# Two gathered steps moved from the v stage to the u stage of a product-key mixer, with later waits on ScalarE and eight weight tiles asked for later

## The chip, the cores and the metric

The kernel runs on one core of one Trainium2 chip. The metric is the device time of one execution in microseconds (us), from the first to the last instruction of the program with what lies around them. Engines are named as in the profile: PE (TensorE matmuls), PEld (its weight loads), DVE (VectorE), ACT (ScalarE), POOL (GpSimd), SP (SyncE, which only issues transfers here). The times below come from three timed executions and from one execution under the profiler.

## The reference

A decoder trunk of two layers over 256 positions of 1024 floats. Layer 0 has an attention and retention mixer, layer 1 a short gated convolution, and each is followed by the channel mixer in which this change lies, an expert retrieval with product keys (PEER):

```python
q = (t @ w_q).reshape(n_tok, PEER_HEADS, 2, PEER_DKEY // 2)          # 8 heads
sc = jnp.einsum('thpd,hpnd->thpn', q, sub_keys)                       # 2 x 128 keys a head
s1, i1 = lax.top_k(sc[:, :, 0], 16)
s2, i2 = lax.top_k(sc[:, :, 1], 16)
cand = s1[..., :, None] + s2[..., None, :]                            # sums of pairs
top_s, pos = lax.top_k(cand, 16)                                      # 16 experts a head
gate = jax.nn.softmax(top_s, axis=-1)
hid = jax.nn.gelu(jnp.einsum('td,thkd->thk', tc, u[ec]))              # rows of u, 16384 x 1024
out = jnp.einsum('thk,thkd->td', gc * hid, v[ec])                     # rows of v, 16384 x 1024
```

So each of 256 tokens needs 128 rows of `u` and the same 128 rows of `v`, with a softmax gate a row. Weights and activations are 32-bit floats.

## The kernel before, in words

**Two ways to the experts.** The first 96 tokens are done by gathering: 96 steps fetch, by an indirect transfer that POOL issues, 128 rows of `u` (one for each partition, 128x1024 floats, 0.524 MB), and DVE multiplies them with the tokens and adds up (line 1043); 96 further steps fetch 128 rows of `v`, which DVE adds into three accumulators with the gate times the hidden value as factor (line 1054). The text calls each of these 192 steps a row. The other 160 tokens go through every expert: the u stage multiplies 128 tiles of `u` (128x1024 floats each) with the tokens on PE (line 1449), ACT applies the gelu (line 1489) and the gates come in later; the v stage multiplies 128 tiles of `v` with the gated hidden values (lines 1555, 1589, 1591). The two ways run side by side: `ga.rate` says how many rows are taken a tile of the u stage, and what is left over is spread evenly over the v stage. `UPTO` is the number of rows, one figure a layer, that are to be done when tile 117 of the u stage is reached (after it the rate is 0.6).

**The order.** Each engine's queue is written out by hand, in the order of the program; nothing is moved by a scheduler. A step of the u stage is: eight double matmuls of tile `i`, the gelu of its 128x160 result on ACT, then whatever the work list (`Pump`) has credit for, then the rows that `ga.rate` has credit for. PE writes the results of successive tiles to four accumulators in turn (`acc` twice, `hid` twice).

**Before the gates.** The work list holds the choice of experts for the 256 tokens in two halves (`th`): the top 16 of each of the 16 score vectors (`stage1`), the candidates of four heads at a time (`stage2_build`, nine broadcast sums after a cast of the indices), their top 16 (`stage2_top`), and the way back from positions to indices (`extract`), all on DVE. Its entries have a cost, and each step gives 1.4 of credit, so an entry `(3.0, None)` is a pause. The softmax is cut in three: `gates` (DVE subtracts the maximum), `gates_exp` (ACT, which loads the table of the exponential for it and then that of the gelu again, lines 1277 and 1489) and `gates_norm` (DVE). The gathered rows have such a pair as well: `later` puts the gelu of 32 hidden values on ACT (line 1049) two rows after the last of them, and the product with the gates on DVE two rows after that. When the list is empty, the gates proper begin: one-hot matrices on DVE, their scaling on ACT (lines 1397 and 1400), small matmuls `G` on PE and a product with the hidden values on DVE (line 1492 for each later tile), in 40 groups over the rest of the u stage.

**Transfers.** SP's queue loads the tiles of `u` and `v` in pairs (1 MB) into a ring of eight tiles, `raw`, each when its place is free. 31 of the 128 tiles of `u` (`PRE`) have places elsewhere, in memory that is not yet or no longer used. Eight of these become free only when the query projection ends, and are asked for at tile 0 (six of them, `early_u`) and at tiles 1 and 2 (`early_ko`).

## Time and profile before

| | |
|---|---|
| median of 3 runs | 1441.81 us (1440.76 to 1442.34) |
| the profiled execution | 1445.61 us, of which the span is 1443.5 us |
| granted PE clock | 0.998 |
| busy share of the span | PE 98%, PEld 93%, DVE 86%, ACT 54%, POOL 49% |
| moved by DMA | 532.28 MB, 369 GB/s over the span |
| u stage, layer 0 and 1 | about 180 to 488 us and 882 to 1185 us from the span's start |
| v stage, layer 0 and 1 | about 488 to 727 us and 1185 to 1425 us |

The rest of the span is the two mixers, the query projections (131 to 180 us and 828 to 882 us) and the last norm. The table of the page says little about the change, since PE looks busy nearly everywhere; the windows by stage and the waits by stage say more. "Waited for" names the instruction that came last before a wait ended. Idle times under 150 ns are not listed among the waits.

### The profile page before, as it was taken

What the parts mean: (1) busy time and instruction counts of PE and PEld (TensorE: products, weight loads), DVE (VectorE), ACT (ScalarE), POOL (GpSimd) and SP (SyncE); (2) the same over time, 40 slices, a digit from 0 to 9 for tenths busy, and PEclk for the clock granted to TensorE, in tenths of its full rate; (3) what the DMA queues carried; (4) which work ended last, traced back from release to release, by engine and by line L of the source; (5) the groups of instructions that cost most, each with busy time, mean ns of one, the idle gap of its engine ahead of it and who ended that gap; (6) DMA issues with size and microseconds to landing.
All of it is one profiled execution on the core that took longest, in us unless ns stands there. A gap on an engine that the chain in (4) does not pass through costs nothing.

```text
span 1443.5 us, 30069 instructions
## 1 busy us (share of the span) xinstructions
PE 1414.7 (98%) x11368; PEld 1343.9 (93%) x11376; DVE 1238.9 (86%) x2520; ACT 775.9 (54%) x1820; POOL 703.0 (49%) x495
## 2 busy tenths in 40 slices
PE   9999999999999999999999999999999999999898
PEld 6679999999999999999999999999999999999897
DVE  6638998978889799999987699998888978999896
ACT  6555412148787455655654452212887845655554
POOL 5753633565555343443236363356665644445440
PEclk9999999999999999999999999999999999999999
DMA  9657899999999999999977599999999999999994
GB/s 371 228 158 255 316 409 396 400 395 413 410 413 404 401 406 415 414 415 414 412 267 238 194 324 377 413 409 383 411 414 412 409 392 412 415 416 414 415 415 173
DMA packets 115361, 532.28 MB, mean 369 GB/s; under 512 B 13008, under 2 KB 13264, under 8 KB 86544
## 3 DMA queue, kind: packets, MB, share of 16 engines
q1 hardware_dynamic: 58320, 325.05, 57.4%
q0 software_dynamic: 56032, 203.74, 35.6%
q8 instruction: 89, 1.46, 0.4%
q10 hardware_dynamic: 864, 1.57, 0.3%
q14 instruction: 56, 0.46, 0.1%
HBM read 528.97 MB, written 1.05 MB: 367 GB/s over the span
## 4 chain that ended last, share of the span: by engine, by line
PE 59%; DMA 17%; DVE 17%; issue 3%; ACT 2%; POOL 1%; DVEq 0%; ACTq 0%; SPq 0%; POOLq 0%
PE hid L1449 25%; PE vo L1589 9%; DMA raw<-pv 8%; DMA rows<-pvn,ig 5%; PE vo L1591 4%; PE hid L324 4%; PE vo L1555 4%; DVE gacc L1054 2%; PE hid L330 2%; DVE vlo L1467 2%; PE G L1407 2%; DVE rows L1043 1%; DMA raw<-ew_in 1%; PE ea L356 1%; PE ea L357 1%
## 5 line engine op out<-in xcount | busy, mean ns | idle before, releaser
L1449 PE MATMUL hid<-xf,raw 128*128 128x160 f32 x3104 | 444.9, 300 | 2.8 <-DVE hg L1492 2.3
L1449 PEld LDWEIGHTS hid<-xf,raw 128*128 128x128 f32 x3104 | 426.3, 190 | 4.0 <-DVE hg L1492 3.3
L1460 ACT CAST vhi<-raw 128x1024 fp32r<-128x1024 f32 x212 | 217.9, 1048 | 197.1 <-DMA raw<-pv 127.8
L1033 POOL DMA_INDIRECT rows<-pvn,ig x128 | 192.2, 1502 | 205.7 <-DVE gacc L1054 159.9
L1467 DVE TENSOR_TENSOR vlo<-raw,vhi 128x1024 bf16<-128x1024 f32 x212 | 255.7, 1220 | 33.9 <-ACT vhi L1460 32.8
L1033 POOL DMA_INDIRECT rows<-pun,ig x128 | 159.6, 1247 | 147.6 <-DVE rows L1043 74.7
L194 POOL TENSOR_TENSOR lo<-raw,hi 128x1024 bf16<-128x1024 f32 x67 | 161.2, 2422 | 83.6 <-ACT hi L190 61.4
L1589 PE MATMUL vo<-ko,vhi 128*128 128x320 f32 x1120 | 199.0, 320 | 0.4 <-ACT vhi L1460 0.4
L1043 DVE SCALAR_TENSOR_TENSOR rows<-rows,xg 128x1024 f32<-128x1024 f32 x128 | 154.8, 1218 | 20.9 <-DMA rows<-pun,ig 20.7
L1589 PEld LDWEIGHTS vo<-ko,vhi 128*128 128x128 f32 x1120 | 165.6, 188 | 1.0 <-ACT vhi L1460 1.0
L1489 ACT ACTIVATE hg<-hid 128x160 f32<-128x160 f32 (+14 forms) x240 | 62.4, 265 | 193.4 <-PE hid L1449 193.2
L1054 DVE SCALAR_TENSOR_TENSOR gacc<-rows,ghid,gacc 128x1024 f32<-128x1024 f32 x124 | 158.5, 1278 | 9.1 <-DMA rows<-pvn,ig 8.9
L1591 PE MATMUL vo<-hb,vlo 128*128 128x160 bf16 x1696 | 154.1, 234 | 8.3 <-DVE vlo L1467 7.9
L1033 POOL DMA_INDIRECT grow<-pvn,ig x64 | 90.1, 1407 | 113.1 <-DVE gacc L1054 88.6
L1591 PEld LDWEIGHTS <-vlo 128*128 128x128 bf16 x1696 | 112.1, 98 | 32.9 <-DVE vlo L1467 13.2
L1397 ACT ACTIVATE ko<-ko,idxT 128x128 f16<-128x128 f16 x320 | 101.7, 391 | 32.4 <-DVE ko L1382 32.2
L190 ACT CAST hi<-raw 128x1024 fp32r<-128x1024 f32 (+1 forms) x101 | 103.3, 1043 | 28.7 <-PE hid L324 16.6
L1555 PE MATMUL vo<-hg,raw 128*128 128x160 f32 x704 | 106.9, 302 | 3.1 <-DVE hg L1492 3.1
L324 PE MATMUL hid<-x,hi 128*128 128x256 f32 x800 | 107.4, 287 | 0.8 <-DVE cg L970 0.8
L1033 POOL DMA_INDIRECT grow<-pun,ig x64 | 73.6, 1150 | 70.8 <-DVE grow L1043 29.3
L1589 PE MATMUL vo<-xf,vhi 128*128 128x320 f32 x576 | 102.5, 320 | 0.4 <-ACT vhi L1460 0.4
L1400 ACT ACTIVATE ko<-ko,idxT 128x128 f16<-128x128 f16 x320 | 101.2, 388 | 0.0
(266 smaller groups left out, 2302.5 us busy)
## 6 DMA issues: line engine op xcount, KB each, us to landing
raw<-pv SPq DMA_DIRECT2D x128, 1024.0 KB, 10.4
raw<-pu SPq DMA_DIRECT2D x96, 1024.0 KB, 8.2
raw<-wq SPq DMA_DIRECT2D x32, 512.0 KB, 4.3
hg<-pe_ SPq DMA_DIRECT2D x28, 512.0 KB, 6.6
raw<-ew_in SPq DMA_DIRECT2D x25, 512.0 KB, 6.0
raw<-ow_in SPq DMA_DIRECT2D x24, 512.0 KB, 5.5
raw<-ew_out SPq DMA_DIRECT2D x8, 512.0 KB, 4.5
raw<-ow_out SPq DMA_DIRECT2D x8, 512.0 KB, 4.5
```

Source lines behind the costliest of these rows:

```text
L190: self.nc.scalar.copy(hi[:, c], t[:, c])
L194: eng.tensor_tensor(lo[:, c], t[:, c], hi[:, c].bitcast(F32), OP.subtract)
L324: pe.matmul(ps[:, :S], hi[:, k * P:(k + 1) * P], A2[:, k, s_, :], start=k == 0 and s_ == 0, stop=False)
L1033: gp.indirect_dma_start(self.row(s_), None, table, bass.IndirectOffsetOnAxis(IG[:, 0, s_ % STEPS:s_ % STEPS + 1].bitcast(U32), 0))
L1043: v.scalar_tensor_tensor(r, r, 1.0, XG[:, 0, :], op0=OP.mult, op1=OP.mult, accum_out=w)
L1054: v.scalar_tensor_tensor(self.acc[q], r, w, self.acc[q], op0=OP.mult, op1=OP.add)
L1449: pe.matmul(ps[:, :TD], w[k], xv["xf"][:, k, :], start=k == 0, stop=k == ND - 1)
L1460: act.copy(whi[j], raw)
L1467: v.tensor_tensor(wlo[j], raw, whi[j].bitcast(F32), OP.subtract)
L1555: pe.matmul(vo[b][:, TG:S], w[:, c], HG[:, i, :], stop=i == NK - 1, **m)
L1589: pe.matmul(vo[b][:, TG:S + TD], hi[:, b * P:(b + 1) * P], hs, **m)
L1591: pe.matmul(vo[b][:, TG:S], lo[:, b * P:(b + 1) * P], hb, **m)
```

## The change

It has five parts.

1. `ga.rate` before the gates is 0.95 rows a tile instead of 0.9 (tiles 8 to 57), and `UPTO` is 123 and 121 instead of 121 and 119: two more rows a layer are done in the u stage, two fewer in the v stage.
2. The candidates of the second token half (`th` = 1) are made by ACT, head by head (`head_build`, nine small activations with a bias, and a cast after the fourth head), in place of two `stage2_build` on DVE. `cand` and `IF` get three buffers instead of one.
3. `gates_exp(0)` comes eight tiles later, `gates_exp(1)` follows `gates(1)` by two pauses instead of one, and the gelu of 32 gathered hidden values comes twelve rows after the last of them instead of two (the product with the gates after sixteen instead of four).
4. The eight tiles of `u` that were asked for at tiles 0, 1 and 2 are asked for one at a time at tiles 2, 10, 16, 21, 26, 31, 36 and 41 (`LATER`), each 24 to 66 tiles before its use.
5. The list of work before the gates is 2.0 shorter in cost (the two builds), so the gates begin sooner.

The same matmuls are made, and the same bytes are moved.

ACT's queue of layer 0 before, from the tiles just ahead of the gelu of the first 32 gathered hidden values (`ghid`) to the exponential of the second token half (`hg` there is the scratch in which the gates lie; `hid` are the accumulators):

```order
L1489 ACTIVATE hg_1301<-hid_2766 128x160
L1489 ACTIVATE hg_1301<-hid_2779 128x160
L1049 ACTIVATE ghid_1306<-ghid_1306 128x32
L1489 ACTIVATE hg_1301<-hid_2794 128x160
L1489 ACTIVATE hg_1301<-hid_2811 128x160
L1489 ACTIVATE hg_1301<-hid_2825 128x160
L1489 ACTIVATE hg_1301<-hid_2839 128x160
L1489 ACTIVATE hg_1301<-hid_2852 128x160
L1277 ACT_TABLE_LOAD
L1277 ACTIVATE hg_1301<-hg_1301,nw_174 128x128
L1489 ACT_TABLE_LOAD
```

The same place now, where the line of the exponential is 1294, of the gelu of a tile 1509 and of `ghid` 1050:

```order
L1509 ACTIVATE hg_1301<-hid_2906 128x160
L1509 ACTIVATE hg_1301<-hid_2918 128x160
L1294 ACT_TABLE_LOAD
L1294 ACTIVATE hg_1301<-hg_1301,nw_174 128x128
L1509 ACT_TABLE_LOAD
L1509 ACTIVATE hg_1301<-hid_2931 128x160
L1509 ACTIVATE hg_1301<-hid_2944 128x160
L1509 ACTIVATE hg_1301<-hid_2956 128x160
L1050 ACTIVATE ghid_1306<-ghid_1306 128x32
L1509 ACTIVATE hg_1301<-hid_2969 128x160
```

The gelu of `ghid` has moved behind the exponential. One of the eight places at which ACT now makes candidates, behind tile 28 of layer 0 (one head is nine activations, lines 1211 and 1212; a cast of the indices follows the fourth and the eighth head):

```order
L1509 ACTIVATE hg_1301<-hid_2618 128x160
L1211 ACTIVATE hg_1301<-hg_1301 128x16
L1211 ACTIVATE hg_1301<-hg_1301 128x8
L1211 ACTIVATE hg_1301<-hg_1301 128x5
L1211 ACTIVATE hg_1301<-hg_1301 128x4
L1211 ACTIVATE hg_1301<-hg_1301 128x3
L1211 ACTIVATE hg_1301<-hg_1301 128x2 x3
L1212 ACTIVATE hg_1301<-hg_1301 128x8
L1509 ACTIVATE hg_1301<-hid_2641 128x160
```

Before, only the gelus stood there, and DVE had nine sums and a cast for four heads at once. SP's queue from the end of the query projection of layer 0, before (the names are where a tile of `u` goes):

```order
L161 DMA raw<-pu 128x2048
L1143 DMA hg_1301<-pe_ 128x1024 x2
L1143 DMA xg<-pe_ 128x1024
L1143 DMA ulo_2101<-pe_ 128x512
L1143 DMA one_1312<-pe_ 128x512
L1143 DMA uhi_2104<-pe_ 128x1024
L1143 DMA uhi_2106<-pe_ 128x1024
L1143 DMA xb<-pe_ 128x1024
L1143 DMA uhi_2109<-pe_ 128x1024
L1143 DMA ulo_2111<-pe_ 128x512
L1143 DMA ulo_2112<-pe_ 128x512
L1143 DMA ko_2130<-pe_ 128x1024 x2
```

and now, up to the fifth of the eight:

```order
L162 DMA raw<-pu 128x2048
L1144 DMA hg_1301<-pe_ 128x1024 x2
L1144 DMA xg<-pe_ 128x1024
L1144 DMA ko_2132<-pe_ 128x1024
L162 DMA raw<-pu 128x2048 x3
L1144 DMA ko_2132<-pe_ 128x1024
L162 DMA raw<-pu 128x2048 x2
L1144 DMA ulo_2372<-pe_ 128x512
L1144 DMA one_1312<-pe_ 128x512
L162 DMA raw<-pu 128x2048 x2
L1144 DMA uhi_2475<-pe_ 128x1024
L162 DMA raw<-pu 128x2048 x2
```

The eight stand between pairs of the ring now, not ahead of all of them. The diff, cut to its core:

```diff
-UPTO = (121, 119)
+UPTO = (123, 121)
...
+LATER = dict(zip((2, 10, 16, 21, 26, 31, 36, 41), [i for i in sorted(PRE) if 14 <= PRE[i] < 22]))
...
-                    self.later[s_ + 2] = lambda: act.activation(w, w, AF.Gelu)
-                    self.later[s_ + 4] = lambda: v.tensor_tensor(w, w, g, OP.mult)
+                    self.later[s_ + 12] = lambda: act.activation(w, w, AF.Gelu)
+                    self.later[s_ + 16] = lambda: v.tensor_tensor(w, w, g, OP.mult)
...
-            IF = scr(half).bitcast(F16)
-            cand = scr(PH // 2 * NC)
+            IF = [scr(half).bitcast(F16) for _ in range(3)]
+            cand = [scr(PH // 2 * NC) for _ in range(3)]
...
-            early_u = [i for i in sorted(PRE) if 14 <= PRE[i] < 20]
-            early_ko = [i for i in sorted(PRE) if 20 <= PRE[i] < 22]
...
+            def part(th, hf):
+
+                return th * (1 + hf)
...
+            def head_build(th, hh):
+                def g():
+                    o = hh * 2 * TK
+                    s1, s2 = V[th][:, o:o + TK], V[th][:, o + TK:o + 2 * TK]
+                    cc = cand[part(th, hh // HH)][:, hh % HH * NC:(hh % HH + 1) * NC]
+                    mid = TK // 2
+                    for a in range(mid):
+                        w = WIDTHS[a]
+                        act.activation(cc[:, STARTS[a]:STARTS[a] + w], s2[:, :w], AF.Identity, bias=s1[:, a:a + 1])
+                    act.activation(cc[:, STARTS[mid]:], s1[:, mid:], AF.Identity, bias=s2[:, 0:1])
+                    if hh % HH == HH - 1:
+                        n = NPAIR * TK // 2
+                        act.copy(IF[part(th, hh // HH)], IU[th][:, hh // HH * n:(hh // HH + 1) * n].bitcast(U32))
+                return g
...
             def chain(th, hf):
-                pump.add((1.0, stage2_build(th, hf)))
+                if th == 0:
+                    pump.add((1.0, stage2_build(th, hf)))
...
-                pump.add(*[(2.7, stage1(1, f, f + 2)) for f in range(HH * 2, NPAIR, 2)])
-                pump.add((0.0, lambda: gates_exp(0)))
+                for h in range(HH):
+                    f = (HH + h) * 2
+                    pump.add((2.7, stage1(1, f, f + 2)), (0.0, head_build(1, h)))
                 chain(1, 0)
+                for h in range(HH):
+                    pump.q.insert(len(pump.q) - 6 + h, (0.0, head_build(1, HH + h)))
+                pump.q.insert(len(pump.q) - 2, (0.0, lambda: gates_exp(0)))
                 pump.add((0.6, lambda: gates_norm(0)), (0.3, shares))
                 chain(1, 1)
-                pump.add((0.3, lambda: gates(1)), (3.0, None), (0.0, lambda: gates_exp(1)), (3.0, None),
-                         (0.6, lambda: gates_norm(1)), (3.0, None), (3.0, None), (0.5, idx_tr), (3.0, None))
+                pump.add((0.3, lambda: gates(1)), (3.0, None), (3.0, None), (0.0, lambda: gates_exp(1)),
+                         (3.0, None), (0.6, lambda: gates_norm(1)), (3.0, None), (0.5, idx_tr), (3.0, None))
...
-                    for k in early_u:
-                        fetch(k)
-                elif early_ko:
-                    fetch(early_ko.pop(0))
+                if i in LATER:
+                    fetch(LATER[i])
...
-                ga.rate = (0.9 if 8 <= i < 58 else 0.6) if gst["g"] < 0 else (UPTO[l] - ga.c) / (NK - CALM - i) if i < NK - CALM else 0.6
+                ga.rate = (0.95 if 8 <= i < 58 else 0.6) if gst["g"] < 0 else (UPTO[l] - ga.c) / (NK - CALM - i) if i < NK - CALM else 0.6
```

More of the change, by code (lines that the diff above doesn't have):

```diff
@@ L1183, in peer @@
             HH = PH // 2
+            def part(th, hf):
+                return th * (1 + hf)
             def stage2_build(th, hf):
                 def g():
-                    hs = slice(hf * HH, (hf + 1) * HH)
                     n = NPAIR * TK // 2
-                    v.tensor_copy(IF, IU[th][:, hf * n:(hf + 1) * n].bitcast(U32))
-                    vv = V[th].rearrange("p (h s k) -> p h s k", h=PH, s=2)[:, hs]
-                    cc = cand.rearrange("p (h n) -> p h n", h=HH)
+                    v.tensor_copy(IF[part(th, hf)], IU[th][:, hf * n:(hf + 1) * n].bitcast(U32))
+                    vv = V[th].rearrange("p (h s k) -> p h s k", h=PH, s=2)[:, hf * HH:(hf + 1) * HH]
+                    cc = cand[part(th, hf)].rearrange("p (h n) -> p h n", h=HH)
                     for a in range(TK // 2):
@@ L1206, in g @@
                         to = (th * PH + hh) * TK
-                        todo.append((top[:, to:to + TK], PU[:, o * TK:(o + 1) * TK], cand[:, o * NC:(o + 1) * NC]))
+                        todo.append((top[:, to:to + TK], PU[:, o * TK:(o + 1) * TK], cand[part(th, h0 // HH)][:, o * NC:(o + 1) * NC]))
                     top16(todo)
@@ L1228, in extract @@
                 hs = slice(hf * HH, (hf + 1) * HH)
-                ii = IF.rearrange("p (h s k) -> p h s k", h=HH, s=2)
+                ii = IF[part(th, hf)].rearrange("p (h s k) -> p h s k", h=HH, s=2)
                 def of(t):
```

## The prediction

> **What bounds the kernel now.** The page says first that PE leaves little:
>
> ```profile
> span 1443.5 us, 30069 instructions
> PE 1414.7 (98%) x11368; PEld 1343.9 (93%) x11376; DVE 1238.9 (86%) x2520; ACT 775.9 (54%) x1820; POOL 703.0 (49%) x495
> ```
>
> So I went to the windows by stage (stretch, length, busy us of PE, PEld, DVE, ACT, POOL, granted clock, DMA share, GB/s), layer 0 and then layer 1:
>
> ```profile
> 180.00:240.00 60.00, 60.00 (x445) 60.00 (x444) 54.93 (x218) 13.27 (x34) 21.31 (x21) 1.00 1.02 409
> 240.00:260.00 20.00, 20.00 (x149) 20.00 (x148) 19.76 (x81) 2.74 (x9) 11.48 (x9) 1.00 0.98 382
> 260.00:280.00 20.00, 19.49 (x144) 19.25 (x143) 19.69 (x75) 2.52 (x10) 12.22 (x13) 1.00 1.02 406
> 280.00:300.00 20.00, 18.17 (x134) 17.93 (x133) 17.16 (x33) 5.08 (x11) 10.44 (x10) 1.00 0.98 383
> 300.00:320.00 20.00, 20.00 (x154) 19.96 (x154) 16.71 (x32) 8.84 (x33) 14.92 (x12) 1.00 1.02 401
> 320.00:476.00 156.00, 154.23 (x1300) 152.03 (x1299) 135.01 (x256) 121.52 (x465) 88.23 (x73) 1.00 1.02 409
> 488.00:727.00 239.00, 234.90 (x2021) 221.66 (x2022) 219.17 (x208) 141.88 (x177) 87.38 (x59) 1.00 1.01 411
> 882.00:980.00 98.00, 98.00 (x724) 98.00 (x723) 95.07 (x372) 17.92 (x51) 41.87 (x41) 1.00 1.02 410
> 980.00:1000.00 20.00, 20.00 (x149) 20.00 (x148) 16.29 (x34) 5.79 (x13) 13.23 (x10) 1.00 0.96 361
> 1000.00:1160.00 160.00, 160.00 (x1349) 158.51 (x1348) 137.01 (x264) 124.98 (x477) 99.97 (x75) 1.00 1.02 412
> 1185.00:1420.00 235.00, 228.89 (x1974) 216.61 (x1975) 218.00 (x207) 139.81 (x175) 102.28 (x61) 1.00 1.01 413
> ```
>
> Three things are to be seen. DMA moves 409 to 413 GB/s all through both stages, except in a hole before the gates (382, 406, 383 and 401 in layer 0, 361 in layer 1): there, as I read it, the ring is full and the rows wait for DVE. DVE is nearly full before the gates (95.07 of 98 us) and in the v stage (219 of 239, 218 of 235). PE idles in layer 0 at 260 to 300 us, and in both v stages. What it waited for there, the waits of PE by stage say (180 to 300, 300 to 488, 488 to 727, 1000 to 1185 and 1185 to 1420 us; in 882 to 1000 there is none):
>
> ```profile
> PE hid L1449 <- ACT hg L1489: 2.3, 2, 1.8
> PE hid L1449 <- DVE hg L1492: 1.8, 3, 1.1
> PE vo L1591 <- DVE vlo L1467: 2.4, 6, 0.7
> PE vo L1555 <- DVE hg L1492: 1.6, 1, 1.6
> PE hid L1449 <- DVE hg L1492: 0.5, 1, 0.5
> PE vo L1591 <- DVE vlo L1467: 5.5, 7, 1.9
> ```
>
> The 2.3 us are two late gelus, and the timeline of ACT has their causes, first in layer 0, then the same two places in layer 1:
>
> ```profile
> 278.68 0.23 ACT L1049 ACTIVATE ghid<-ghid 128x32 f32<-128x32 f32 x1 [8.39 <-DVE rows L1043]
> 281.95 1.28 ACT L1277 ACT_TABLE_LOAD   x1
> 290.04 0.40 ACT L1277 ACTIVATE hg<-hg,nw 128x128 f32<-128x128 f32 x1 [6.81 <-DVE hg L1273]
> 290.46 1.28 ACT L1489 ACT_TABLE_LOAD   x1
> ...
> 964.90 0.30 ACT L1489 ACTIVATE hg<-hid 128x160 f32<-128x160 f32 x1 [1.87 <-PE hid L1449]
> 967.07 0.30 ACT L1489 ACTIVATE hg<-hid 128x160 f32<-128x160 f32 x1 [1.87 <-PE hid L1449]
> ...
> 977.09 0.23 ACT L1049 ACTIVATE ghid<-ghid 128x32 f32<-128x32 f32 x1 [5.37 <-DVE rows L1043]
> 988.45 0.40 ACT L1277 ACTIVATE hg<-hg,nw 128x128 f32<-128x128 f32 x1 [4.57 <-DVE hg L1273]
> ```
>
> DVE runs behind the program, and ACT, in order, stands on it with gelus queued behind. In layer 1 waits of 5.37 and 4.57 us cost PE nothing (98.00 of 98, 20.00 of 20), in layer 0 8.39 and 6.81 us cost 2.3: with four accumulators and a tile every 2.17 us (964.90 to 967.07), PE bears some 3 x 2.17 = 6.5 us. That layer 0 is later has a row of its own: in 180 to 300 us DVE waited 4.2 us for gathers, and the chain of waits has one that took 14 us, while the eight early tiles (4.2 MB, about 10 us at 410 GB/s) stood ahead of it:
>
> ```profile
> L1043 DVE SCALAR_TENSOR_TENSOR grow<-grow,xg 128x1024 f32<-128x1024 f32 x14 | 17.0, 1214 | 4.2 <-DMA grow<-pun,ig 4.2
> 210.26 13.96 DMA grow<-pun,ig
> ```
>
> **The change part by part.** All sums are against the profiled span of 1443.5 us. Its execution took 1445.61 us, 3.8 us over the median of 1441.81, so a difference is carried over to the median as it is.
>
> *ACT's later waits.* Both waits of layer 0 should go. The exponential now comes five tiles after its input was put on DVE's queue (before: two); the three more are 6.5 us, against a wait of 6.81. The gelu of `ghid` comes ten rows later, about ten tiles or 22 us, against 8.39. Gain: 2.3 us in layer 0, none in layer 1. Above: 2.3; below: 0, where what PE wins it then waits for data.
>
> *Candidates on ACT.* One build on DVE:
>
> ```profile
> 198.61 0.22 DVE L1189 CAST hg<-hg 128x128 f16<-128x128 uint32 x1
> 198.75 0.83 DVE L1194 TENSOR_TENSOR hg<-hg 128x64 f32<-128x64 f32 x8
> 199.49 0.18 DVE L1197 TENSOR_TENSOR hg<-hg 128x32 f32<-128x32 f32 x1
> ```
>
> about 1.1 us from 198.61 to 199.67; two leave DVE a layer, 2.2 us. On ACT come 72 activations of 2 to 16 elements and two casts a layer. No such activation is in the trace; the nearest are 0.23 us (128x32, above) and 0.40 us (128x128 with a scale by partition), so a head costs 9 x 0.23 = 2.1 to 9 x 0.40 = 3.6 us. I take 2.1, the tiles being small. The place is empty enough: ACT is busy 17.92 of 98 us in 882 to 980. Four heads stand at every second tile: 2.1 + 0.3 in 4.3 us. The other four stand at tiles 26 to 29, with a cast (0.4) and the exponential with two table loads (1.28 + 0.40 + 1.28 = 3.0) at the end: 4 x 2.4 + 3.4 = 13.0 us in 4 x 2.17 = 8.7, so ACT ends 4.3 us late, under 6.5. At 3.6 a head it is 10.3 us late, and PE stands 3.8 us a layer. New waits on DVE: the last head needs a top 16 that was put on DVE's queue eight tiles (17 us) before. DVE's lag at 270 us was about the 8.39 of the wait and the two tiles before it, 13 us. That holds with 4 us to spare. Cost 0, above 3.8 a layer.
>
> [...] What it could cost is the 3.8 us a layer above, 0.02 of the chances. [...]
>
> *Two rows sooner.* A row on DVE is 1.21 us before the gates and 1.28 in the v stage:
>
> ```profile
> L1043 DVE SCALAR_TENSOR_TENSOR rows<-rows,xg 128x1024 f32<-128x1024 f32 x28 | 33.6, 1215 | 1.6 <-DMA rows<-pun,ig 1.6
> L1054 DVE SCALAR_TENSOR_TENSOR gacc<-rows,ghid,gacc 128x1024 f32<-128x1024 f32 x42 | 53.7, 1278 | 0.6 <-DMA rows<-pvn,ig 0.5
> L1467 DVE TENSOR_TENSOR vlo<-raw,vhi 128x1024 bf16<-128x1024 f32 x105 | 126.5, 1221 | 18.2 <-ACT vhi L1460 17.8
> ```
>
> Forty tiles at 0.05 more are two rows: 2.4 us on DVE, which the builds pay with 2.2; and 2 x 0.524 MB, 2.5 us at 412 GB/s. The v stage has 2.6 us less on DVE and 2.5 us less to load. It is short of both: DVE waits 17.8 us for ACT's `vhi`, which waits for `raw`. Alone, that would take up to 2.5 us of 2.4 in layer 0 and of 5.5 in layer 1.
>
> But the bytes must then be loaded sooner, and DMA has no room except in the hole. This decides the sum. Against 412 GB/s the hole of layer 0 is (30 + 6 + 29 + 11) x 20 us = 1.52 MB or 3.7 us, that of layer 1 51 x 20 us = 1.02 MB or 2.5 us: about three rows and two. From tile 8, 0.95 rows and about 0.75 ring tiles each 2.17 us ask for 410 GB/s, before 398: the higher rate closes the hole by itself.
>
> *The eight tiles.* The same bytes, later by up to 41 tiles (89 us). They leave the stretch at 180 to 200 us, where the rows of layer 0 waited, and fall into the hole, the last four at about 239, 250, 261 and 272 us. They stand 24 tiles (52 us) or more ahead of their use: cost 0. DVE regains up to 3 of its 4.2 us in layer 0.
>
> *Sooner gates.* 2.0 of cost at 1.4 a tile: the 40 groups begin about two tiles earlier, with the same work. 0.
>
> *The sum.* Layer 0: above 3.7 us (the hole; ACT's 2.3 are part of it, since PE gives back what it gains without bytes), below 2.3; I take 3.0. Layer 1: above 2.5, below 0, as PE has no wait before its gates; I take 2.0, since the rate closes the hole on any path. Together 5.0: span 1438.5, median 1441.8 - 5.0 = 1436.8.
>
> **The rivals.** *More than the hole.* If the v stages starve by bunching and not by bytes, two rows fewer might free all their waits for `vlo`, 2.4 and 5.5 us, with ACT's 2.3: 10.2 us, 1431.6. For it: layer 1's longest wait is 1.9 us, a few events. Against it: 411 to 413 GB/s throughout.
>
> *Nothing.* The hole opens elsewhere: without the burst DMA runs dry at 200 to 240 us, layer 0's gain of 2.3 comes back as waits for `raw`, and layer 1 has two rows more to load before its v stage. For it: bytes are the same, and the ring is empty where the v stages begin. About 1 us, 1440.8. New waits of ACT on DVE would end here too.
>
> *Slower: DVE late in the gate stage.* There it makes one-hots, products and 1.2 rows a tile, and is busy 135 of 156 us while waiting for rows; PE already waits 1.8 and 0.5 us for line 1492. The gates begin two tiles (4.3 us) sooner, with two rows more done in that time. If DVE has not caught up by then, it goes in 4.3 us late and each layer's wait grows by that: +8.6, less the 2.3 and some 2 of the v stages: +4.3, 1446.1. It decides where DVE's lag at the first group is over about 4 us. Against it: the pauses before the gates are kept, and in 300 to 320 us DVE idles 3.3 of 20.
>
> **How the numbers follow.** What this kernel's measurement can tell from no change is about 0.2%, 2.9 us. The forecast has 0.50 (own range 1434 to 1439), more than the hole 0.13, nothing 0.23, slower 0.14 (DVE late 0.12, ACT's heads at 3.6 us 0.02). The forecast's edge gives 0.02 to no change: faster 0.61, same 0.25, slower 0.14. The range leaves out half of the first rival and the worse half of the slower one: 1432 to 1444.
>
> **What would show it.** Right: no wait of ACT for lines 1043 or 1273 over 1 us; 405 GB/s or more at 240 to 300 and at 980 to 1000 us; PE without waits for ACT in 180 to 300; fewer us of waits for `vlo` in both v stages; two casts and 18 sums fewer on DVE a layer. ACT's heads near 2.1 us. Wrong: a new hole at 200 to 240; waits of PE for line 1492 over 3 us a layer (the slower rival); waits for `vlo` as before with the hole closed.

## The result, and the profile after

| | before | changed |
|---|---|---|
| median of 6 runs | 1441.68 us (1439.74 to 1444.02) | 1453.50 us (1449.87 to 1457.64) |
| the profiled execution, its span | 1445.61, 1443.5 us | 1452.58, 1450.8 us |
| mean granted PE clock | 0.998 | 0.994 |

The ratio of changed to before is 1.0069, with a 95% interval of 1.0043 to 1.0096: slower by 10 us by the ratio (the medians are 11.8 us apart), where 5 us less had been forecast. The profiled execution of before took longer than any of its six others, so the spans show 7.3 us of it.

The same windows as before, of the changed kernel (stretch, length, busy us of PE, PEld, DVE, ACT, POOL, granted clock, DMA share, GB/s):

```profile
180.00:210.00 30.00, 30.00 (x224) 30.00 (x223) 28.58 (x133) 6.04 (x17) 9.72 (x10) 1.00 0.88 322
240.00:260.00 20.00, 20.00 (x150) 20.00 (x149) 18.16 (x66) 12.42 (x49) 9.49 (x7) 1.00 1.02 414
260.00:280.00 20.00, 20.00 (x150) 20.00 (x149) 15.71 (x59) 2.74 (x9) 8.54 (x9) 1.00 1.02 408
280.00:300.00 20.00, 16.86 (x105) 16.62 (x105) 17.28 (x30) 4.88 (x11) 10.44 (x10) 0.84 1.02 412
488.00:727.00 239.00, 236.55 (x2029) 223.07 (x2028) 219.03 (x208) 143.55 (x182) 98.32 (x59) 1.00 1.01 409
882.00:912.00 30.00, 30.00 (x226) 29.95 (x224) 28.48 (x134) 5.85 (x17) 9.72 (x10) 1.00 0.85 316
980.00:1000.00 20.00, 16.58 (x115) 16.34 (x114) 17.64 (x38) 4.88 (x11) 11.99 (x9) 0.92 1.02 410
1185.00:1420.00 235.00, 229.86 (x1970) 217.21 (x1969) 213.36 (x205) 138.52 (x177) 99.92 (x62) 1.00 1.01 409
```

and the two stretches of before that the prediction showed only as part of longer ones:

```profile
180.00:210.00 30.00, 30.00 (x224) 30.00 (x223) 28.58 (x133) 6.04 (x17) 9.68 (x10) 1.00 1.02 407
882.00:912.00 30.00, 30.00 (x224) 30.00 (x223) 28.62 (x132) 5.51 (x16) 9.96 (x11) 1.00 1.03 410
```

The hole before the gates is filled (382 to 414 GB/s at 240 us, 361 to 410 at 980), as the prediction wanted. A new one is there at the start of the stage (407 to 322, 410 to 316). DVE, which before was full at 240 to 280 us (39.45 of 40 us), is now busy 33.87, and the two builds that it no longer makes are 2.2 of that. And PE, which had lost 2.3 us to ACT in layer 0 and nothing in layer 1, stands over 3 us in each layer, and then runs at a lower clock. The timelines of ACT and of PE show the place, layer 0 and then layer 1:

```profile
292.73 0.40 ACT L1294 ACTIVATE hg<-hg,nw 128x128 f32<-128x128 f32 x1 [8.12 <-DVE hg L1290]
293.15 1.28 ACT L1509 ACT_TABLE_LOAD   x1
995.79 0.40 ACT L1294 ACTIVATE hg<-hg,nw 128x128 f32<-128x128 f32 x1 [8.40 <-DVE hg L1290]
```

```profile
294.80 7.44 PE L1471 MATMUL hid<-xf,raw 128*128 128x160 f32 x32 [3.13 <-ACT hg L1509]
997.86 6.40 PE L1471 MATMUL hid<-xf,raw 128*128 128x160 f32 x24 [3.42 <-ACT hg L1509]
```

The exponential (line 1277 of before, now 1294) still waits for DVE, 8.12 us instead of 6.81, although it stands three tiles later in ACT's queue. Its wait, itself (0.40) and a table load (1.28) come to 9.8 us, 3.3 more than the 6.5 us that four accumulators bear, and PE stood 3.13. Then comes a second loss: 32 matmuls take 7.44 us; at the usual rate they take 4.51, as before from 294.39 us on. The granted clock says why, in windows of 4 us:

```profile
292.00:296.00 4.00, 1.20 (x4) 1.20 (x5) 2.98 (x6) 2.69 (x7) 2.25 (x2) 0.72 1.02 416
296.00:300.00 4.00, 4.00 (x16) 4.00 (x16) 2.94 (x5) 0.30 (x1) 2.15 (x3) 0.50 1.01 400
300.00:304.00 4.00, 4.00 (x29) 4.00 (x29) 3.90 (x7) 0.30 (x1) 3.39 (x3) 0.92 1.01 388
```

In layer 1 the clock is 0.50 over 999 to 1003 us. So each layer loses some 3.3 us of waiting and 2.9 us of slow matmuls, about 12 us in all on PE, where before it had lost 2.3.

### The profile page after: what moved, and what is told of

Read it like the earlier page. It is cut to its first block, busy times and chain, and to the rows that moved or that the text cites. A ratio compares the mean times of both kernels' runs of the same rounds, so it can differ in the third digit from the quotient of the medians.

```text
span 1450.8 us, 30181 instructions
## 1 busy us (share of the span) xinstructions
PE 1423.5 (98%) x11376; PEld 1349.6 (93%) x11376; DVE 1236.0 (85%) x2484; ACT 805.2 (55%) x1972; POOL 715.5 (49%) x495
## 4 chain that ended last, share of the span: by engine, by line
PE 44%; DVE 23%; DMA 22%; issue 7%; ACT 2%; POOL 1%; DVEq 0%; ACTq 0%; SPq 0%; POOLq 0%
PE hid L1471 15%; DMA raw<-pv 10%; PE vo L1609 7%; DMA rows<-pun,ig 6%; PE vo L1575 4%; PE vo L1611 4%; DVE vlo L1489 3%; DMA grow<-pun,ig 3%; PE hid L325 3%; DVE gacc L1055 2%; DVE rows L1044 2%; PE G L1429 2%; DVE hg L1157 2%; DVE hg L1163 1%; DVE hg L1159 1%
## 5 line engine op out<-in xcount | busy, mean ns | idle before, releaser
L1471 PE MATMUL hid<-xf,raw 128*128 128x160 f32 x3104 | 451.6, 303 | 7.5 <-ACT hg L1509 6.6
L1471 PEld LDWEIGHTS hid<-xf,raw 128*128 128x128 f32 x3104 | 432.0, 192 | 9.4 <-ACT hg L1509 7.0
L1034 POOL DMA_INDIRECT rows<-pvn,ig x128 | 181.3, 1417 | 214.4 <-DVE gacc L1055 171.1
L1034 POOL DMA_INDIRECT rows<-pun,ig x128 | 156.3, 1221 | 161.2 <-DVE rows L1044 60.2
L1509 ACT ACTIVATE hg<-hid 128x160 f32<-128x160 f32 (+15 forms) x240 | 62.6, 264 | 182.7 <-PE hid L1471 158.2
L1034 POOL DMA_INDIRECT grow<-pvn,ig x64 | 107.6, 1681 | 99.1 <-DVE gacc L1055 75.6
L1034 POOL DMA_INDIRECT grow<-pun,ig x64 | 82.5, 1289 | 57.7 <-DVE grow L1044 17.1
```

The source lines that it names most:

```text
L1034: gp.indirect_dma_start(self.row(s_), None, table, bass.IndirectOffsetOnAxis(IG[:, 0, s_ % STEPS:s_ % STEPS + 1].bitcast(U32), 0))
L1471: pe.matmul(ps[:, :TD], w[k], xv["xf"][:, k, :], start=k == 0, stop=k == ND - 1)
```

## The experiments

The texts on record speak of theories. A: the eight late tiles do it. B: the 0.95 rows a tile do it. C: a wait that is taken away at one place only moves. D: late gathers hold up DVE, and through it PE. E: bytes that DMA does not move at 180 to 210 us are lost for good. F: such bytes cost nothing up to the size of the old hole. G: every late tile costs alike. H: the landing time of a gather against six row buffers. All ratios are to the kernel before, run on the same chip, with a 95% interval; each trace is of one execution. Diffs are cut to their core, and `...` marks what is left out.

### Which part of the change

**The tiles early again, the rest as changed.**

```diff
...
                 if i == 0:
                     after_first()
-                if i in LATER:
-                    fetch(LATER[i])
+                    for k in early_u:
+                        fetch(k)
+                elif early_ko:
+                    fetch(early_ko.pop(0))
```

> The changed kernel, with the eight tiles asked for at tiles 0, 1 and 2 again. Theory A (the tiles that are asked for later leave DMA idle at 180 to 210 us and crowd the gathers at 240 to 290 us; DVE falls 20 us behind and ACT's second exponential waits 8 us for it): 400 GB/s or more at 180 to 210, that wait under 3 us, no stall of PE over 1 us before the gates, no drop of the granted clock; 1434 to 1440 us, 12 to 18 under the changed kernel. Theory B (0.95 rows a tile are more than DVE and DMA bear): the wait of about 8 us and the stall of 3 us remain, 1448 to 1454 us.

Measured 1444.72 us, 1.0010 (0.9996 to 1.0024). The first hole is gone (406 and 410 GB/s), ACT's waits are down to about 2 us, and the clock does not fall in the traced execution (0.998; the other nine have 0.994 to 0.998). So A holds against B. But the gain did not come: PE now waits at the transposes of the indices, which the trace of before did not show as a wait (timeline of PE, layer 0 and layer 1):

```profile
301.94 0.33 PE L1336 MATMUL it<-cst,hg 128*128 128x128 f32 x1 [3.50 <-DVE hg L1304]
1000.38 0.33 PE L1336 MATMUL it<-cst,hg 128*128 128x128 f32 x1 [2.23 <-DVE hg L1304]
```

The changed list has one pause between DVE's norm (line 1304) and these transposes, where before it had two.

**The late tiles alone, on the kernel before.** The diff above the other way round, with `LATER`.

> The kernel before, with only the eight tiles asked for later. Theory A: DVE falls behind by 4 to 8 us more than before, and the second exponential, which comes two tiles after its input here, waits 11 to 15 us instead of 6.8 and 4.6; PE stalls 5 to 8 us a layer and its clock drops: 1455 to 1465 us. Theory B: as before, 1439 to 1444 us.

Measured 1457.39 us, 1.0101 (1.0081 to 1.0120), with 317 and 316 GB/s at the start of the stages, a stall of PE of 4.22 us in layer 0 with a fall of the clock behind it (0.83 over 280 to 300 us), and two waits of 5.2 us together in layer 1 without one (1.00 from 980 to 1020 us). The late tiles alone cost no less than the whole change.

**The old row rate, the rest as changed.**

```diff
-UPTO = (123, 121)
+UPTO = (121, 119)
...
-                ga.rate = (0.95 if 8 <= i < 58 else 0.6) ...
+                ga.rate = (0.9 if 8 <= i < 58 else 0.6) ...
```

> The changed kernel with 0.9 rows a tile and 121 and 119 rows in the u stage, as before. Theory A: little changes before the gates, the wait of ACT is 6 to 8 us and PE's stall 1 to 3 us; two rows a layer come back to the v stage: 1446 to 1454 us. Theory B: wait and stall vanish, 1438 to 1442 us.

Measured 1454.29 us, 1.0081 (1.0060 to 1.0102): nothing is regained, B falls. The waits are not where A put them: ACT's exponential waits 4.1 and 4.2 us, and PE stands 6.4 and 6.6 us at the transposes.

**The other three parts, each alone on the kernel before.** The two rows (the diff above the other way round), ACT's heads (the changed kernel with the rows, the later waits and the late tiles taken back), and ACT's later waits with the changed list, of which the core is:

```diff
-                    self.later[s_ + 2] = lambda: act.activation(w, w, AF.Gelu)
+                    self.later[s_ + 12] = lambda: act.activation(w, w, AF.Gelu)
...
-                pump.add((0.0, lambda: gates_exp(0)))
                 chain(1, 0)
+                pump.q.insert(len(pump.q) - 2, (0.0, lambda: gates_exp(0)))
...
-                pump.add((0.3, lambda: gates(1)), (3.0, None), (0.0, lambda: gates_exp(1)), (3.0, None),
-                         (0.6, lambda: gates_norm(1)), (3.0, None), (3.0, None), (0.5, idx_tr), (3.0, None))
+                pump.add((0.3, lambda: gates(1)), (3.0, None), (3.0, None), (0.0, lambda: gates_exp(1)),
+                         (3.0, None), (0.6, lambda: gates_norm(1)), (3.0, None), (0.5, idx_tr), (3.0, None))
```

> The kernel before with 0.95 rows a tile and totals of 123 and 121 rows alone, nothing else of the change. The prediction's step (two rows fill the hole before the gates): 1441.7 less 3 to 5, 1437 to 1439. From the pair of kernels with both places mended, where the rate made 0 (1.0013 against 0.9999): 1441 to 1444. If DVE gets late before the gates: 1445 or more, with the waits of ACT for ghid and the exponential above 8.4 and 6.8.

> The kernel before with the candidates of the second half built a head at a time on ACT, nothing else of the change. The prediction's step: cost 0 and 2.2 us a layer less on DVE, so waits of ACT on DVE before the gates 1 to 2 us shorter and the time equal or up to 1.5 us less, 1440 to 1442. If the heads make ACT late: gelus behind them late, new waits of PE for L1509-like gelus at 210 to 260 us, 2 to 4 us a layer more.

> The kernel before with ACT's later waits alone: ghid's gelu ten rows later, the first exponential later, and the changed list (the pause from ahead of the transposes put ahead of the second exponential). The prediction's step: both waits of layer 0 go, 2.3 us of PE: 1439.4. With what the kernel with early tiles showed: the waits at ACT go, but PE waits 3 us in layer 0 and 2 in layer 1 at the transposes of the indices, 1441 to 1445.

Measured 1.0009 (0.9991 to 1.0027), 1.0001 (0.9987 to 1.0015) and 1.0001 (0.9983 to 1.0018). None of the three moves the time by what can be told from nothing. The rows did not close the hole, they moved part of it (windows of the kernel with the rows alone; before: 382, 406, 383 and 401 GB/s), and PE's waits for ACT grew to 3.9 us in layer 0 and 2.7 in layer 1 (before 2.3 and none):

```profile
240.00:260.00 20.00, 20.00 (x150) 20.00 (x149) 19.76 (x84) 2.73 (x9) 10.05 (x10) 1.00 1.01 399
260.00:280.00 20.00, 18.79 (x139) 18.55 (x138) 19.71 (x75) 2.49 (x10) 11.53 (x12) 1.00 1.02 408
280.00:300.00 20.00, 17.31 (x127) 17.07 (x126) 16.95 (x32) 4.80 (x11) 10.61 (x10) 1.00 0.96 368
300.00:320.00 20.00, 19.97 (x150) 19.30 (x148) 15.33 (x30) 5.67 (x22) 12.80 (x10) 1.00 0.99 379
```

The later waits do end PE's 2.3 us of waits for ACT in layer 0, but PE then waits 1.88 and 1.39 us at the transposes of the indices, as above.

### Can the list of pauses mend it?

**The second exponential one pause later, the rest as changed.**

```diff
-(0.3, lambda: gates(1)), (3.0, None), (3.0, None), (0.0, lambda: gates_exp(1)),
+(0.3, lambda: gates(1)), (3.0, None), (3.0, None), (3.0, None), (0.0, lambda: gates_exp(1)),
```

> The changed kernel with one more pause (2.1 tiles, 4.7 us) between the gates of the second token half and their exponential. Under A and B alike DVE is as late as in the changed kernel, and only what ACT does with it differs: the wait falls from 8.1 to 8.4 us to about 3.5, PE has no stall of 3 us and the granted clock stays at 1.00 in 280 to 304 us. If stall and slow clock are the whole loss (3.3 + 2.9 us a layer), 12 us come back: 1440 to 1443. If DVE's lateness costs by itself (late gates, ring behind), 1446 or more.

Measured 1458.66 us, 1.0104 (1.0083 to 1.0125). ACT's waits are short now (2.8 and 1.4 us), and PE stands 9.66 and 9.21 us at the transposes.

**Tiles early and two pauses again ahead of the transposes; the same with the old rate.** The tiles as in the first experiment, and the list:

```diff
-(0.3, lambda: gates(1)), (3.0, None), (3.0, None), (0.0, lambda: gates_exp(1)),
-(3.0, None), (0.6, lambda: gates_norm(1)), (3.0, None), (0.5, idx_tr), (3.0, None))
+(0.3, lambda: gates(1)), (3.0, None), (3.0, None), (0.0, lambda: gates_exp(1)),
+(0.6, lambda: gates_norm(1)), (3.0, None), (3.0, None), (0.5, idx_tr), (3.0, None))
```

> The changed kernel with the eight tiles asked for at tiles 0, 1 and 2 again, and the list of the gates with two pauses again between the norm and the transposes of the indices (gates, pause, pause, exponential, norm, pause, pause, transposes, pause), still five. Theory A (tiles and list): the loss sits in the postponed tiles, and what the kernel with early tiles alone still lost was the pause that the list takes away before the transposes, where PE waited 3.50 and 2.23 us. Then no wait of PE there over 1 us, no drop of the granted clock, and 1444.7 - 5.7 = 1439.0, ratio about 0.997, span 1436 to 1438. Rival C (the wait only moves): the exponential and the norm now stand together, DVE's norm waits for the exponential and PE or ACT waits elsewhere as long, 1443 to 1446.

> The same kernel as the one with both places mended, with 0.9 rows a tile and the old totals (121 and 119 rows), so without the two rows sooner. The prediction's hole (two rows fill a hole of 3.7 and 2.5 us): the two rows are worth about 2.5 to 5 us, so this one is 2.5 to 5 us slower than its pair, DMA at 240 to 300 us falls to the 382 to 401 GB/s of before. Rival (bytes are the same, the loads are only moved): within 1.5 us of its pair. Rival (two rows more make DVE late before the gates): this one is faster than its pair by 1 to 3 us.

Measured 1445.34 us, 1.0013 (0.9995 to 1.0032), and 1443.05 us, 0.9999 (0.9981 to 1.0018). The transposes no longer wait. In the first of the two the wait stands at the first group of the gates instead, behind the one-hot matrices that DVE makes between rows (`PE G <- ACT ko`, 2.31 us in layer 0, with a fall of the clock behind it, 0.85 over 300 to 320 us); with the old rate 0.7 us of it are left. C was right about the time. The two rows are worth nothing here either.

**Tiles late, seven pauses.** The list of the changed kernel with three pauses ahead of the exponential and three between norm and transposes.

> The changed kernel, its eight tiles late, with seven pauses: three ahead of the exponential and three between the norm and the transposes. If the late tiles cost only through the two waits of PE and the clock that falls after them, both waits are gone or under 2 us, the clock stays, and the time is 1453.5 - 12.4 = 1441 (1440 to 1443), equal to before. If DVE's and DMA's lateness costs by itself, it comes out as PE waits in the gate stage (the gates begin two tiles later) or in the v stage, and the time stays at 1446 or more.

Measured 1454.54 us, 1.0063 (1.0045 to 1.0081): no stall before 320 us, and then one of 4.91 us (layer 1: 5.23) at the first group of the gates, with the clock down behind it (0.98 over 320 to 476 us, 0.96 over 1020 to 1160). With late tiles, DVE was late at each of the three places to which the list put the wait: the exponential, the transposes and the gates.

**Tiles late, fewer rows before the gates.**

```diff
-                ga.rate = (0.95 if 8 <= i < 58 else 0.6) ...
+                ga.rate = (0.8 if 8 <= i < 58 else 0.6) ...
```

> The changed kernel, its eight tiles late, with 0.8 instead of 0.95 rows a tile before the gates (tiles 8 to 57) and the same 123 and 121 rows by the end of the u stage: some 7 rows (3.9 MB) are asked for after the gates have begun instead of before. The kernels with late tiles have each lost about 12 us whatever the list of pauses. Theory D (late gathers): from 210 us on DMA has more asked of it than 412 GB/s, so gathers come later and later, and whatever stands behind a row on DVE (norm, shares of the indices) makes PE wait. With fewer rows the gathers are in time: no wait of PE over 1.5 us and no drop of the clock at 270 to 330 and 975 to 1030 us, and the time goes back to 1441 to 1446. Theory E (lost bytes): the 30 us at 320 instead of 407 GB/s are 2.6 and 2.8 MB that DMA never gets back, 6.2 + 6.8 = 13 us; then the gates may run clean, but the same time is lost after them as waits for raw, vlo or rows, and it stays at 1450 or more.

Measured 1454.95 us, 1.0088 (1.0066 to 1.0111). PE runs clean up to 320 us, as D said, and the time does not come back, as E said: the rows put off must be done after the gates have begun. PE waits 5.1 us in layer 0 and 4.5 in layer 1 for DVE's products with the gates (line 1512; before 1.8 and 0.5), and the clock falls once in each layer there (0.65 over 378 to 382 us, 0.54 over 1083 to 1086). The same rate with early tiles was not run, so how much of the 1.0088 the lower rate costs by itself is not known.

### Lost bytes, or late gathers

**The eight tiles not loaded, in the changed kernel and in the kernel before.** These two leave out the loads; the matmuls of the eight tiles take the weights of another tile that is there.

```diff
                 k = PRE[i]
+                if 14 <= k < 22:
+                    there[i] = [EX[:, 0, c:c + P] for c in range(0, D, P)]
+                    return
```

> The changed kernel with the eight tiles not loaded at all: their matmuls take the weights of another early tile that is there, so the output is not the reference's and everything else is as in the changed kernel, its 320 GB/s at 180 to 210 us too. Theory E (lost bytes): what those 30 us lose is not their idle DMA time in itself but that 4.2 MB a layer still have to go over a DMA that is full from then to the end of the v stage; without them 10.2 us a layer less, 1453.5 - 20.4 = 1433 (1430 to 1437, PE's own work being the floor), without waits at the gates and without a drop of the clock. Theory D (the order in which gathers and tiles come) would leave part of it: rows start as they did, 1441 or more. If the tiles' place is only a matter of the gates' waits: 1453.5 less the 12 of stalls and clock, 1441.

> The kernel before with the same eight tiles not loaded, in the same way: its output is not the reference's. It now has the 320 GB/s at 180 to 210 us of the changed kernel. Theory E: of the 10.2 us of DMA a layer that the tiles take, 6.5 lay in a stretch that would have been idle anyway, so leaving them out is worth only 3.7 us a layer: 1441.7 - 7.4 = 1434 (1431 to 1438), the same as the changed kernel without them, within 3 us. If an idle DMA at 180 to 210 us harms by itself, it is slower than before: 1445 or more.

Measured 1443.04 us, 1.0001 (0.9987 to 1.0016), and 1440.50 us, 0.9987 (0.9974 to 1.0000). E is not borne out: with some 10 us of DMA a layer less (4.2 MB at 410 GB/s), the one is level with the kernel before and the other 1.9 us under it (the interval ends at 1.0000). DMA idles at 180 to 210 us in both (299 and 303 GB/s), and it does no harm where there is that much less to load. So an idle DMA there is no loss in itself; the tiles harm where they are put. PE was 98% busy before, so a gain of 10 us a layer may have had no room to show, and these two kernels alone do not exclude E. A second row speaks against it: in the v stages of the changed kernel, where bytes that are missing should starve PE, it waits 2.0 and 3.6 us for `vlo`, before 2.4 and 5.5. The second kernel also gives an estimate of what a placing of these tiles that disturbs nothing could bring: 1.9 us.

**How many tiles.** Three and five late, the others at tiles 0, 1 and 2:

```diff
-LATER = dict(zip((2, 10, 16, 21, 26, 31, 36, 41), ...))
+LATER = {31: 82, 36: 92, 41: 107}
+LATER = {21: 66, 26: 76, 31: 82, 36: 92, 41: 107}   (the second kernel)
```

> The changed kernel with three of the eight tiles late (the last three, at tiles 31, 36 and 41) and five at tiles 0, 1 and 2. The two ends stand: none late 1444.7, eight late 1453.5. Theory F (a reserve): before the gates DMA runs into full buffers anyway and loses 3.7 and 2.5 us there, so bytes that come later cost nothing until they fill that, 1.57 MB or 3.8 us here, of which 180 to 210 us loses 1 MB at most: 1444 to 1446, DVE's lag of rows at 270 us as with early tiles (14.6 us). Theory G (each late tile delays gathers by its own 1.3 us of DMA): linear, 3/8 of 8.8 us, 1448.0, lag between 14.6 and 20.5 us.

> The changed kernel with five of the eight tiles late (at tiles 21, 26, 31, 36 and 41) and three at tiles 0, 1 and 2. Theory F: 2.6 MB late, of which some 1 to 1.5 MB (2.5 to 3.7 us) are lost at 180 to 210 us, about the reserve of layer 0 and 1 us over that of layer 1: 1445 to 1447. Theory G: 5/8 of 8.8 us, 1450.2.

Measured 1449.78 us, 1.0034 (1.0008 to 1.0059), and 1452.26 us, 1.0074 (1.0057 to 1.0091). F falls: with three late, 180 to 210 us loses hardly anything (397 and 388 GB/s), and it still costs 1.0034. G is nearer, some 2 us under both; but eight cost no more than five.

**The tiles spread, but early** (one a tile at tiles 1 to 8, with the mended list):

```diff
-LATER = dict(zip((2, 10, 16, 21, 26, 31, 36, 41), ...))
+LATER = dict(zip((1, 2, 3, 4, 5, 6, 7, 8), ...))
```

> The kernel with both places mended, its eight tiles asked for one a tile at tiles 1 to 8, not in a burst at 0, 1 and 2 and not up to tile 41. If what hurts is that DMA runs dry at 180 to 210 us, this one keeps 400 GB/s there and has the time of its pair within 1.5 us. If a burst is bad for the first rows (the prediction's 14 us gather behind the burst), it is faster than its pair by 1 to 2 us and DVE's waits for gathers in 180 to 300 us fall under 4.2. If any postponing starves the ring, the rate at 180 to 210 us is under 400 and it is 2 us or more slower than its pair.

Measured 1452.47 us, 1.0044 (1.0025 to 1.0063): slower than its pair with the burst by 7 us in the medians. DVE is starved earlier here, 24.35 us busy of 30 at 210 to 240 us where its pair is busy 28.09.

What goes with the time in these kernels, all with 0.95 rows a tile and six buffers for rows, is DVE's lag: from the end of the last matmul of tile 41 to the start on DVE of the row that stands in that tile's step, worked out from the starts of rows and matmuls in each trace.

| kernel | lag in layer 0 and 1, us | ratio |
|---|---|---|
| eight tiles not loaded | 12.3, 12.5 | 1.0001 |
| early, mended list | 13.9, 13.2 | 1.0013 |
| early, changed list | 14.6, 14.5 | 1.0010 |
| the two rows alone | 15.1, 13.8 | 1.0009 |
| three late | 15.6, 17.0 | 1.0034 |
| spread at tiles 1 to 8 | 17.9, 17.8 | 1.0044 |
| five late | 20.0, 19.5 | 1.0074 |
| the changed kernel | 20.5, 20.8 | 1.0069 |
| late, seven pauses | 20.7, 20.8 | 1.0063 |
| late, exponential one pause later | 21.7, 20.4 | 1.0104 |

Each lag is of one execution and each ratio of all. Three late took 1453.84 us when traced and five late 1449.14, against the order of their lags; the mean granted clock of these two executions was 0.994 and 0.998, and 0.004 of 1450 us is an estimated 6 us. So the lag parts the kernels into two groups, up to 15.1 us and from 15.6 us on, and within the second the falls of the clock count as well. Nor is the lag before the gates the whole loss: with late tiles and 0.8 rows a tile it is 9.6 and 9.5 us, under the 13.5 and 10.5 of the kernel before, and the ratio is still 1.0088.

**What makes DVE late.** The view of transfers gives, for the gathers that fell into 225 to 280 us, their number and the median us from issue to landing: first of before, then of the late tiles with seven pauses, and last of the late tiles with 0.8 rows a tile. For the changed kernel it gives the number alone, 12 and 7; the second of the three has its rate and, up to the second exponential, its order.

```profile
rows<-pun,ig POOLq DMA_INDIRECT x14, 9.5
grow<-pun,ig POOLq DMA_INDIRECT x8, 9.9
```

```profile
rows<-pun,ig POOLq DMA_INDIRECT x12, 15.0
grow<-pun,ig POOLq DMA_INDIRECT x7, 14.1
```

```profile
rows<-pun,ig POOLq DMA_INDIRECT x12, 13.4
grow<-pun,ig POOLq DMA_INDIRECT x8, 13.5
```

The tiles stand in DMA among the gathers (in the changed kernel six of their loads are issued in the same 55 us as 19 of them), and these land 4 to 5.5 us later. At the same 0.95 rows a tile it is 9.0 and 9.5 us with the tiles early and the mended list, and 8.5 and 10.2 with the tiles not loaded, so it is the tiles and not the rate. In the changed kernel DVE waits for that in the same 55 us (waits of DVE; before it is one wait of 1.6 us):

```profile
DVE rows L1044 <- DMA rows<-pun,ig: 3.8, 4, 1.6
DVE grow L1044 <- DMA grow<-pun,ig: 2.5, 3, 1.3
```

There are six buffers for rows, two `grow` and four `rows`, and one is free again only when POOL has issued the gather, it has landed and DVE has used the row. In the changed kernel POOL waits 7.4 and 5.2 us for rows on DVE at 225 to 280 us, and one of its issues there takes 0.94 us:

```profile
238.68 0.94 POOL L1034 DMA_INDIRECT grow<-pun,ig  x1 [1.21 <-DVE hg L1155]
```

With DVE's 1.2 us for a row, at 9.5 us that is 0.9 + 9.5 + 1.2 = 11.6 us a round, a row each 1.9 us; wanted is one each 2.17 / 0.95 = 2.28. At 15.0 and 14.1 us (about 14.7 over the 19) it is 16.8, a row each 2.8 us, so each row comes 0.5 us later than wanted. The changed kernel bears this out: DVE's lag grew from 10.7 us at tile 20 to 20.5 at tile 41, which is 20 rows, and 6.3 us of it are listed waits for gathers. With 0.8 rows a tile the round is 15.5 us, a row each 2.6, and wanted is one each 2.7: there the lag stays at 9.6 us. To test this without moving a byte:

**Five row buffers, tiles early, mended list.**

```diff
-MORE = 4
+MORE = 3
```

> The kernel with both places mended (eight tiles early, 0.95 rows a tile; 1445.3, ratio 1.0013), with five buffers for gathered rows instead of six. Theory H (slots and landing time): a row is wanted every 2.17 / 0.95 = 2.28 us; six buffers allow a gather 13.7 us from its issue to the end of its row on DVE, five 11.4. With early tiles a gather of 225 to 280 us lands in 9.0 to 9.5 us, and with DVE's 1.2 and POOL's 1 us before the issue that is 11.5: six buffers cover it, five do not. Then DVE waits for gathers at 225 to 280 us with the tiles early (0 waits with six buffers, 6.3 us in the changed kernel), its lag grows to 17 us or more, PE waits 3 us or more at the gates, and the time is 1449 to 1458, although no byte is moved. If what counts is only the bytes that DMA does not move at 180 to 210 us: 400 GB/s or more there, and 1445 to 1447.

Measured 1468.92 us, 1.0177 (1.0160 to 1.0194). DMA moves 410 GB/s at 180 to 210 us and gathers land as fast as with six buffers (8.9 and 9.9 us), yet DVE waits for them at 225 to 280 us:

```profile
DVE rows L1044 <- DMA rows<-pun,ig: 2.4, 2, 2.2
DVE grow L1044 <- DMA grow<-pun,ig: 2.0, 3, 1.0
```

Its lag at tile 41 is 19.1 us in layer 0 and 15.6 in layer 1 (with six buffers 13.9 and 13.2), and PE stands 7.13 and 5.49 us at the first group of the gates. So fewer buffers alone bring waits for gathers, the lag and the stall, as H said. The size was well over what H said: five buffers are short in the gate stage too (373 GB/s at 320 to 476 us, before 409; PE waits 6.8 us for the products there in layer 0), so this kernel does not price the stretch before the gates by itself. Seven buffers were not tried.

No kernel of the study that loads all its tiles beats the kernel before; the best of them lie within what can be told from nothing.

## Why the prediction was wrong, point by point

**The step that failed** is the one on the eight tiles: "They stand 24 tiles (52 us) or more ahead of their use: cost 0. DVE regains up to 3 of its 4.2 us in layer 0." Alone they cost 1.0101, some 14 us. The step asked whether the tiles come in time for their own use, and they do. It did not ask who stands behind them in DMA. It took the hole before the gates for free room, and gave it twice, to the two rows and to the tiles. That hole is where DVE was full (39.45 of 40 us at 240 to 280 us). Filled with tiles, it lengthens the landing of a gather from 9.5 to 15 us, past what six buffers cover at 0.95 rows a tile; DVE's lag grows to 20.5 us, PE stands over 3 us in each layer and its clock falls to 0.50.

What the step said of the start was right. Before, DVE waited for gathers twice at 180 to 225 us, and in the changed kernel not at all:

```profile
DVE grow L1043 <- DMA grow<-pun,ig: 1.6, 1, 1.6
DVE rows L1043 <- DMA rows<-pun,ig: 1.6, 1, 1.6
```

These 3.2 us were regained, and at 225 to 280 us 6.3 were lost where before 1.6 were. (The prediction counted 4.2 us of such waits before, those for `grow` alone; with the 1.6 for `rows` that its own lines show it is 5.8.)

**The bound.** PE's waits for ACT in layer 0 and their causes were read rightly, and so were the 6.5 us that PE bears: ACT 9.8 us late left PE 3.13 us. "DMA has no room except in the hole" asked for bytes alone; what starved DVE here is the time of a round through a buffer, which grows when tiles stand between the gathers (from 11.6 us to 16.8, both worked out above from landing times of 9.5 and 14.7 us).

**ACT's later waits: 2.3 us.** The waits went when the tiles were early, and the gain went to a wait that the prediction did not look for. The list was read as two pauses ahead of the exponential instead of one; that the pause was taken from between the norm and the transposes of PE was not weighed. Alone: 1.0001.

**Candidates on ACT: cost 0.** Right. In the changed kernel a head is this, eight sums of up to 16 elements and a ninth:

```profile
239.74 1.61 ACT L1211 ACTIVATE hg<-hg 128x16 f32<-128x16 f32 x8
241.25 0.29 ACT L1212 ACTIVATE hg<-hg 128x8 f32<-128x8 f32 x1
```

That is 1.8 us from 239.74 to 241.54, where 2.1 was taken. What was thought to come of it, DVE's 2.2 us a layer, cannot be told from nothing alone: 1.0001.

**Two rows sooner: 5.0 us.** Nothing that can be told from noise: 1.0009 alone, 1.0013 against 0.9999 in the mended pair. This term carried most of the sum of 5.0 us, and with the tiles early the gain did not come either (1.0010). That "the higher rate closes the hole by itself" is wrong: alone, the rows shrink the hole at 240 us (382 to 399 GB/s) and deepen it at 280 to 320 us (368 and 379). The direction for the v stages was right in layer 1: waits for `vlo` are 3.6 us in the changed kernel and 3.5 with the rows alone, before 5.5. In layer 0 (2.0 and 1.6, before 2.4) it is less clear. It is too little to show in the time.

**The rivals.** "Nothing" named the very sign that came, DMA dry without the burst, but priced it at what it costs in bytes, about 1 us; it appeared at 180 to 210 us, not 200 to 240. The slower rival had the right engine and sign, DVE late at the gates, and the wrong cause (sooner gates) and place: it looked at the products of line 1492, where the changed kernel's waits fell from 1.8 and 0.5 to 0.5 us and none that is listed. Its point of decision, a lag of DVE of over 4 us, was the right quantity, but it was not asked what the tiles do to it. None of them held that PE's clock falls behind a stall, as it did here (0.50 over 296 to 300 us). The step on sooner gates (0) was not tried apart; nothing in the gate stage of the changed kernel speaks against it.

**Open.** How the 10 us of the changed kernel split into waits, slow clock and DVE's lateness after the gates was not separated. The kernels that took away the waits before the gates lost the same time behind them, so PE's waits of 3 us are where the loss shows. That the late tiles are its source is shown by the kernels with the tiles early or not loaded; that they act through late gathers rests on the landing times, DVE's waits and the kernel with five buffers, and no run shortened the landing with the tiles left late. Why eight late tiles cost no more than five was not tested.

## What to carry to other kernels

A prefetch that is "in time for its use" can still cost (the eight late tiles alone 1.0101): ask which transfers that an engine waits for one by one (here the gathers) share DMA with it where it is put, and whether buffers divided by round time still give the rate that is wanted. An early burst into a stretch where DMA has little else to do (322 and 316 GB/s at the start of the changed kernel's stages) was worth 7 us more here, in the medians, than a spread over tiles 1 to 8. Where an engine lags behind, look down the queue for the next place that needs it before counting the gain of a later wait: here, with late tiles, PE stood 3.13 us behind the exponential, 9.66 us at the transposes when the exponential came later, and 4.91 us at the gates when both did.

## What the hardware showed that was not expected

In the changed kernel PE's granted clock was 0.50 at 296 to 300 us, behind a stall of 3.13 us that ended at 294.80, and the matmuls there took 2.9 us more than usual. In the kernel with late tiles and 0.8 rows a tile, the clock fell behind a stall of 2.31 us (0.65 over 378 to 382 us; 16 matmuls in 4.12 us, usual 2.34):

```profile
378.95 4.12 PE L1471 MATMUL hid<-xf,raw 128*128 128x160 f32 x16 [2.31 <-DVE hg L1512]
388.25 2.34 PE L1471 MATMUL hid<-xf,raw 128*128 128x160 f32 x16
```

while in the kernel with early tiles a stall of 3.50 us from 298.44 us left it at 1.00:

```profile
296.00:300.00 4.00, 2.44 (x19) 2.19 (x18) 1.26 (x3) 0.79 (x5) 1.00 (x2) 1.00 1.03 421
300.00:304.00 4.00, 2.06 (x15) 2.06 (x16) 2.54 (x6) 0.83 (x3) 2.62 (x2) 1.00 1.00 411
```

So the length of a stall alone does not say here whether the clock falls. What else decides it, no run shows.
